# Sums for the odd output weights: moved from the mixing stage into the query and key stage, at two steps a piece

## The chip, the cores and the metric

One core of a Trainium2 chip runs the whole kernel. The metric is the device time of one execution in microseconds (us). TensorE (PE) multiplies, VectorE (DVE) and ScalarE (ACT) prepare operands and empty PSUM, and every transfer between device memory and on-chip memory is issued by one queue, that of SyncE (SP). Each engine runs its own list of instructions strictly in order, and so does SP: a transfer that has to wait holds up all that stand behind it.

## The reference, cut to what matters

Two residual layers over 1024 tokens of width 1024, batch 1, all in float32.

```python
def even_layer(x, cos, sin, mem_n, ...):          # layer 0
    proj = rmsnorm(x, g_norm) @ w_in              # 1024 x 6656
    qk, v_a, x_b, q_m, z = split(proj)            # qk: 3 dilations x (query, key) x 4 heads x 128
    a_out = dilated_attention_mixer(qk, v_a, cos, sin)
    b_out = multiscale_pool(x_b, w_pool, pool_scale)
    m_out = memory_attention(q_m, mem_n, w_mem_kv)
    return x + (concat(a_out, b_out, m_out) * silu(z)) @ w_out     # w_out: 1536 x 1024

def odd_layer(x, mem_n, ...):                     # layer 1
    u, v, q_m, z = split(rmsnorm(x, g_norm) @ w_in)
    c_out = chunked_spatial_gating(u, v, ln_g, ln_b, w_s, b_s)     # the "mixing" of chunks of 128 tokens
    m_out = memory_attention(q_m, mem_n, w_mem_kv)
    return x + (concat(c_out, m_out) * silu(z)) @ w_out            # w_out: 1536 x 1024
# the end: rmsnorm(x, final_norm_g)
```

## The kernel before

**Products.** A float32 matmul is made of three passes over operands that are split into a high and a low part: high times high, high times low, low times high. `split` makes the parts: ACT writes the high part (line 111, tile `wh`), DVE subtracts to get the low part (line 112, tile `wl`). On top of that, the large products use a seven-product scheme in place of eight block products. For that, sums and differences of weight blocks and of activation blocks are needed.

**Pairs.** The input projections go in pairs of 128 output columns. `pair` issues one pair: seven products in the order 1, 7, 6, 4, 5, 2, 3, each of 12 matmuls of 128x128x512 (4 slices of depth, 3 passes), so 84 matmuls. After each product one *step* runs (`step`), and each step advances a few generators by one `yield`: the preparation of the next pair's weights (`prep_steps`: four sums `sw` in lines 147 to 161, seven splits), the two side generators `side[0]` and `side[1]`, and the attention units. DVE empties the PSUM banks (tiles `pj`) of a pair in four instructions: `u` or `u2` (line 278) after product 6, `X` (line 282) after product 4, `X` (line 286) after product 5, `X` (line 291) after product 2. Product 3 adds into the bank that line 286 reads, so it cannot start before that instruction is done. The raw weights of a pair come in two transfers of 512 KB (`raw_pair`, line 107), two pairs ahead, into three buffers.

**Stages.** After the memory keys come the query and key stage (six batches of two pairs, here pairs 0 to 11; `project_batch`), the attention stage of layer 0 (its first pairs are called pairs 12 and 13 here, tiles `xb` and `zb`), the output product of layer 0, the value product of layer 1, a memory stage, the mixing stage of layer 1 (four rounds `g` = 0, 2, 4, 6 of two pairs each; `mixed` is side generator 1) and the output product of layer 1. In the query and key stage the rotation of a batch (`rotate`: a shuffle in line 708 and three instructions in lines 710, 712 and 714) is side generator 1 of the batch behind it.

**Sums of output weights.** The output products and the value product use the seven-product scheme too. The sums of their weights are made ahead and put into device memory (`wt_d`, `ws_d`), from where the later stages read them. `sums_of` does this in pieces of 512 KB: two loads of 256 KB into a tile `wt`, four DVE instructions of 128x256 (line 204), one store of 512 KB. There are two `wt` buffers, so the load of piece n+2 waits until the store of piece n has landed. There are 8 pieces for the value product, 12 for the even output weights and 12 for the odd ones. The first 20 are side generator 0 of the query and key stage, the last 12 that of the mixing stage. A piece takes three steps: one yield after the loads, one after two of the four sums, one after the store. Below, o0 to o11 are the odd pieces in their order.

**What sets the order.** The code is written for all engines at once; the framework that lowers it then lists each engine's instructions by its own estimate of when each is ready. So a change in one place can move instructions of any engine that stand near it. The lists are fixed before the run.

Of the kernel before, what the change touches and what calls it, by code (L numbers as in the profile page):

```python
# [47 lines left out]
def trunk(ctx, tc, A):  # L48
# [4 lines left out]
    def pool(name, side="left"):  # L53
        st = ExitStack()
        return st, st.enter_context(tc.tile_pool(name=name, bufs=1, side=side, reuse_waits="tile"))
# [24 lines left out]
    def at(t, off, ap):  # L80
        return bass.AP(tensor=t.tensor, offset=t.offset + off, ap=ap)
# [92 lines left out]
    H1 = ((4, 5, 6, 7, 0, 1), (8, 9, 10, 11, 2, 3))  # L174
    H2 = ((8, 9, 10, 11, 0, 1), (2, 3, 4, 5, 6, 7))
    sub, add = OP.subtract, OP.add

    def out_pieces(l, w, h):
        for j in range(6):
            for c in range(2):  # L180
                src = [at(w, h[q][j] * 131072 + c * 256, [[1024, 128], [512, 2], [1, 256]]) for q in range(2)]
                dst = at(wt_d, ((l * 6 + j) * 128) * 2048 + c * 256, [[2048, 128], [512, 4], [1, 256]])
                yield src, dst, ((3, 3, 1, sub), (1, 1, 0, sub), (0, 3, 0, add), (2, 2, 0, sub))

    def v_pieces(w):
        for c in range(2):
            for q in range(4):
                src = [at(w, h * 524288 + c * 131072 + q * 256, [[1024, 128], [262144, 2], [1, 256]]) for h in range(2)]
                dst = at(ws_d, c * 524288 + q * 256, [[4096, 128], [1024, 4], [1, 256]])
                yield src, dst, ((3, 2, 3, add), (2, 0, 2, sub), (0, 3, 0, sub), (1, 1, 0, sub))  # L190

    def sums_of(p, pieces):
        prev = None
        for src, dst, f in chain(pieces, ((None, None, None),)):
            t = None
            if src:
                t = p.tile([128, 4, 256], F32, name="wt", tag="wt", bufs=2)
                for q in range(2):
                    D.dma_start(t[:, 2 * q:2 * q + 2, :], src[q])
            yield  # L200
            if prev:
                tt, dd, ff = prev
                for n, (o, x, y, op) in enumerate(ff):
                    V.tensor_tensor(tt[:, o, :], tt[:, x, :], tt[:, y, :], op=op)  # L204
                    if n == 1:
                        yield
                D.dma_start(dd, tt)
                yield
            prev = (t, dst, f)

    side = [iter(()), iter(())]
# [90 lines left out]
    def pair_tiles(p, src, idx, tag, bufs, permuted=False):  # L302
        xs = [p.tile([128, 1024], F32, name="X", tag=tag, bufs=bufs) for _ in range(2)]

        def dst(blk, half):
            if permuted:
                d = xs[blk].rearrange("p (r q) -> p r q", r=4)[:, :, half * 128:half * 128 + 128]
                return d, lambda t: t.rearrange("p (q r) -> p r q", r=4)
            return xs[blk][:, half * 512:(half + 1) * 512], lambda t: t
        pair(src, idx, dst)  # L310
        return xs
# [348 lines left out]
    sq, pq = pool("pq", "right")  # L660
# [43 lines left out]
    def rotate(bi, g, C, S_):  # L704
# [10 lines left out]
        for i in range(4):  # L715
            D.dma_start(qk_d[bi, i, 96:128, :], g[i * 32:(i + 1) * 32, :])

    sums = sums_of(pq, chain(v_pieces(A["wov"]), out_pieces(0, A["woute"], H1)))
    for bi in range(6):
        side[1] = project_batch(bi, rope_tables if bi == 0 else None)  # L720
        if bi == 0:
# [159 lines left out]
    def y_out(p, l, r, o, z):  # L881
        t = gate(p, z, "t", 2)
        V.scalar_tensor_tensor(o, o, 0.5, t, op0=OP.mult, op1=OP.mult)
        D.dma_start(y_d[l][r], o)
# [116 lines left out]
    def out_first(p, w, h):  # L1001
        return [to_ops(p, "ow", OW, half_raw(w[h[0][j], :, :512])) for j in range(6)]
# [275 lines left out]
    def mixed(g, out):  # L1278
        vgs = []
        for q in range(2):  # L1280
            vg = pc_.tile([128, 8, 128], F32, name="vg", tag="vg", bufs=2)
            D.dma_start(vg, at(v2_d, (g + q) * 128, [[1024, 128], [128 * 1024, 8], [1, 128]]))
            vgs.append(vg)
        yield
        for q, vg in enumerate(vgs):
            for n in range(8):
                V.tensor_scalar(vg[:, n, :], vg[:, n, :], lr[:, 0, n:n + 1], lr[:, 1, n:n + 1], op0=OP.mult, op1=OP.add)
            mx = pc_.tile([128, 8, 128], F32, name="mx", tag="mx", bufs=2)
            out.append(mx.rearrange("p n t -> p (n t)"))
            yield  # L1290
            for a in range(2):
                pm_ = bank(("s", "s", "tr", "pv")[q * 2 + a])
                for n in range(4):
                    T.matmul(pm_[:, n * 128:(n + 1) * 128], vg[:, a * 4 + n, :], wsT[:, g + q, :], start=True, stop=True)
                V.scalar_tensor_tensor(mx[:, a * 4:a * 4 + 4, :], pm_.rearrange("p (n t) -> p n t", n=4),
                                       smalls[:, 4 + g + q:5 + g + q], Bg[:, g + q:g + q + 1, :].to_broadcast([128, 4, 128]),
                                       op0=OP.mult, op1=OP.add)
                yield

    spre, ppre = pool("ppre", "right")  # L1300
    side[0] = sums_of(ppre, out_pieces(1, A["wouto"], H2))
    mx = []
    side[1] = mixed(0, mx)
    next(side[1])
    for g in range(0, 8, 2):
        us = pair_tiles(pb, A["wo"], (g, g + 1), "X", 4)
        for _ in side[1]:
            pass
        for q in range(2):
            V.tensor_tensor(us[q], us[q], mx[q], op=OP.mult)  # L1310
        if g < 6:
            mx = []
            side[1] = mixed(g + 2, mx)
            next(side[1])
        if g == 6:
            for _ in side[0]:
                pass
            spre.close()
            sc.close()
            sr.close()  # L1320
            sln.close()
            sw_, pw = pool("ow1", "right")
            first = out_first(pw, A["wouto"], H2)
        for q, z in enumerate(pair_tiles(pb, A["wo"], (12 + g, 13 + g), "X", 4)):
            y_out(pb, 1, g + q, us[q], z)
# [86 lines left out]
```

## Time and profile before

| | |
|---|---|
| three timed runs | 1290.73, 1290.88 and 1292.93 us, median 1290.88 us |
| the profiled execution | 1293.09 us in all, 1291.1 us of it the span from the first to the last instruction |
| PE busy | 1249.8 us (97%), 6008 matmuls |
| DVE busy | 1043.2 us (81%) |
| ACT busy | 578.5 us (45%) |
| transfers | 226.10 MB, 52.6% of the time of the 16 DMA engines |

Busy time of PE says little of its pace, since a matmul starts before the one ahead of it has ended: matmuls of 128x128x512 last 0.39 us each and start every 0.23 us. What PE loses shows as a longer distance between two starts. A row of the timeline has the start, the duration, the engine, the line, the operation, the tiles as out<-in, and in brackets, where the engine sat idle ahead of it, for how long and until what.

### The profile page before, as it was taken

What the parts mean: (1) busy time and instruction counts of PE and PEld (TensorE: products, weight loads), DVE (VectorE), ACT (ScalarE), POOL (GpSimd) and SP (SyncE); (2) the same over time, 40 slices, a digit from 0 to 9 for tenths busy, and PEclk for the clock granted to TensorE, in tenths of its full rate; (3) what the DMA queues carried; (4) which work ended last, traced back from release to release, by engine and by line L of the source; (5) the groups of instructions that cost most, each with busy time, mean ns of one, the idle gap of its engine ahead of it and who ended that gap; (6) DMA issues with size and microseconds to landing.
All of it is one profiled execution on the core that took longest, in us unless ns stands there. A gap on an engine that the chain in (4) does not pass through costs nothing.

```text
span 1291.1 us, 17491 instructions
## 1 busy us (share of the span) xinstructions
PE 1249.8 (97%) x6008; PEld 1024.2 (79%) x6008; DVE 1043.2 (81%) x1968; ACT 578.5 (45%) x1155; POOL 48.3 (4%) x51
## 2 busy tenths in 40 slices
PE   6999999999999999999999999999999999999997
PEld 6888888788877877787788787877888887888786
DVE  5998777877676787887977967998878999667976
ACT  6734323233345554455553644632656232243552
POOL 1162000000000000000000001000000000000001
PEclk9999999999999999999999999999999999999999
DMA  7824765767447656533259534524032677239633
GB/s 271 286 99 135 249 207 177 224 198 243 147 149 223 221 161 223 183 114 112 77 191 347 179 108 182 194 96 131 18 98 89 201 240 236 66 115 334 236 114 130
DMA packets 128990, 226.10 MB, mean 175 GB/s; under 512 B 11139, under 2 KB 79363, under 8 KB 128902
## 3 DMA queue, kind: packets, MB, share of 16 engines
q1 hardware_dynamic: 128902, 224.99, 52.6%
q8 instruction: 47, 0.77, 0.3%
q14 instruction: 41, 0.34, 0.1%
HBM read 158.79 MB, written 63.01 MB: 172 GB/s over the span
## 4 chain that ended last, share of the span: by engine, by line
PE 61%; DVE 18%; DMA 13%; issue 4%; ACT 2%; POOL 1%; SPq 1%; DVEq 0%; POOLq 0%; ACTq 0%
PE pj L265 33%; DMA raw<-wt_d 2%; DVE wl L112 2%; DMA sl<-qk_d 2%; PE pv L490 2%; PE pj L432 2%; PE pj L433 2%; PE pj L434 2%; PE s L465 2%; DMA raw<-in_we_dram 1%; PE s L777 1%; DMA ct<-rr_d 1%; PE pj L1045 1%; DVE wt L204 1%; PE pj L1043 1%
## 5 line engine op out<-in xcount | busy, mean ns | idle before, releaser
L265 PE MATMUL pj<-hTh,wh 128*128 128x512 f32 x544 | 217.7, 400 | 6.1 <-DVE u L278 4.2
L265 PE MATMUL pj<-hTh,wl 128*128 128x512 f32 x544 | 215.1, 396 | 0.0
L265 PE MATMUL pj<-hTl,wh 128*128 128x512 f32 x544 | 213.8, 393 | 0.0
L111 ACT ACTIVATE wh<-sw 128x512 fp32r<-128x512 f32 x136 | 85.8, 631 | 220.7 <-PE pj L265 184.6
L111 ACT ACTIVATE wh<-raw 128x512 fp32r<-128x512 f32 x106 | 66.8, 630 | 147.0 <-PE pj L265 136.8
L265 PEld LDWEIGHTS pj<-hTh,wh 128*128 128x128 f32 x544 | 102.6, 189 | 30.2 <-DVE u L278 6.7
L112 DVE TENSOR_TENSOR wl<-sw,wh 128x512 fp32r<-128x512 f32 x136 | 93.3, 687 | 32.8 <-ACT wh L111 31.5
L265 PEld LDWEIGHTS pj<-hTh,wl 128*128 128x128 f32 x544 | 102.6, 189 | 20.9
L265 PEld LDWEIGHTS pj<-hTl,wh 128*128 128x128 f32 x544 | 102.7, 189 | 19.6
L111 ACT ACTIVATE owh<-raw 128x512 fp32r<-128x512 f32 x84 | 52.3, 628 | 79.0 <-DMA raw<-wt_d 36.5
L112 DVE TENSOR_TENSOR owl<-raw,owh 128x512 fp32r<-128x512 f32 x84 | 57.4, 690 | 34.0 <-ACT owh L111 33.8
L112 DVE TENSOR_TENSOR wl<-raw,wh 128x512 fp32r<-128x512 f32 x106 | 72.6, 685 | 8.9 <-ACT wh L111 7.7
L1045 PE MATMUL pj<-owh,oyl 128*128 128x512 f32 x192 | 76.3, 398 | 0.9 <-DVE oyl L112 0.9
L1043 PE MATMUL pj<-owh,oyh 128*128 128x512 f32 x192 | 76.4, 398 | 0.0
L1044 PE MATMUL pj<-owl,oyh 128*128 128x512 f32 x192 | 75.7, 394 | 0.0
L204 DVE TENSOR_TENSOR wt<-wt 128x256 f32<-128x256 f32 x128 | 51.6, 421 | 9.1 <-DMA wt<-in_woute_dram 2.6
L265 PE MATMUL pj<-t2h,wh 128*128 128x512 f32 x136 | 54.5, 401 | 0.0
L265 PE MATMUL pj<-t0l,wh 128*128 128x512 f32 x136 | 53.8, 395 | 0.0
L265 PE MATMUL pj<-t0h,wh 128*128 128x512 f32 x136 | 53.7, 395 | 0.0
L265 PE MATMUL pj<-t2l,wh 128*128 128x512 f32 x136 | 53.6, 394 | 0.0
L265 PE MATMUL pj<-t1h,wh 128*128 128x512 f32 x136 | 53.5, 394 | 0.0
L377 POOL TENSOR_TENSOR rs<-ss,nhalf 128x1 f32<-128x1 f32 x18 | 12.0, 668 | 1108.0 <-DVE ss L376 1108.0
(364 smaller groups left out, 3098.1 us busy)
## 6 DMA issues: line engine op xcount, KB each, us to landing
raw<-in_we_dram SPq DMA_DIRECT2D x44, 512.0 KB
wt_d<-wt SPq DMA_DIRECT2D x24, 512.0 KB
y<-y_d SPq DMA_DIRECT2D x24, 512.0 KB
raw<-wt_d SPq DMA_DIRECT2D x48, 256.0 KB
raw<-in_wo_dram SPq DMA_DIRECT2D x24, 512.0 KB
y_d<-X SPq DMA_DIRECT2D x20, 512.0 KB
qk_d<-X SPq DMA_DIRECT2D x24, 384.0 KB
sl<-qk_d SPq DMA_DIRECT2D x16, 512.0 KB
```

The costliest lines, as they stand in the source:

```text
L111: S.activation(hi, raw, AF.Copy)
L112: e.tensor_tensor(lo, raw, hi.bitcast(F32), op=OP.subtract)
L204: V.tensor_tensor(tt[:, o, :], tt[:, x, :], tt[:, y, :], op=op)
L265: T.matmul(ps, w[:, k, :], m, start=(start and k == 0 and w is hi and m is B[k][0]), stop=(k == 3 and w is lo), skip_group_check=True)
L432: T.matmul(ps, hi, wh[c], start=(k == 0), stop=False)
L433: T.matmul(ps, hi, wl[c], start=False, stop=False)
L434: T.matmul(ps, lo, wh[c], start=False, stop=(k == 7))
L465: T.matmul(s3[:, a, :], qs[i][:, (pr * 2 + a) * 128:(pr * 2 + a + 1) * 128], kvp[j][:, :256], start=n == 0, stop=n == 2)
L490: T.matmul(pv[:, pr * 256:(pr + 1) * 256], kvp[i][:, 256 + kb * 128:384 + kb * 128], PT[j][:, kb * 256:(kb + 1) * 256], start=(kb == 0 and ...
L1043: T.matmul(ps, yh[:, c], wh, start=start, stop=False, skip_group_check=True)
L1044: T.matmul(ps, yh[:, c], wl, start=False, stop=False, skip_group_check=True)
L1045: T.matmul(ps, yl[:, c], wh, start=False, stop=stop, skip_group_check=True)
```

## The change

`sums_of` loses its first yield, so that a piece takes two steps: the loads of piece n+1 and the first half of the sums of piece n in one, the second half and the store of piece n in the next. The 12 odd pieces join the chain of the query and key stage (32 pieces in all, with the same two `wt` buffers), and the mixing stage has no side generator 0 any more, nor the pool that it used and the loop that ran it dry ahead of the last round. The arithmetic of each piece is the same.

```diff
--- before.py
+++ after.py
@@ -197,7 +197,6 @@
                 t = p.tile([128, 4, 256], F32, name="wt", tag="wt", bufs=2)
                 for q in range(2):
                     D.dma_start(t[:, 2 * q:2 * q + 2, :], src[q])
-            yield
             if prev:
                 tt, dd, ff = prev
                 for n, (o, x, y, op) in enumerate(ff):
@@ -715,7 +714,7 @@
         for i in range(4):
             D.dma_start(qk_d[bi, i, 96:128, :], g[i * 32:(i + 1) * 32, :])
 
-    sums = sums_of(pq, chain(v_pieces(A["wov"]), out_pieces(0, A["woute"], H1)))
+    sums = sums_of(pq, chain(v_pieces(A["wov"]), out_pieces(0, A["woute"], H1), out_pieces(1, A["wouto"], H2)))
     for bi in range(6):
         side[1] = project_batch(bi, rope_tables if bi == 0 else None)
         if bi == 0:
@@ -1297,8 +1296,6 @@
                                        op0=OP.mult, op1=OP.add)
                 yield
 
-    spre, ppre = pool("ppre", "right")
-    side[0] = sums_of(ppre, out_pieces(1, A["wouto"], H2))
     mx = []
     side[1] = mixed(0, mx)
     next(side[1])
@@ -1313,9 +1310,6 @@
             side[1] = mixed(g + 2, mx)
             next(side[1])
         if g == 6:
-            for _ in side[0]:
-                pass
-            spre.close()
             sc.close()
             sr.close()
             sln.close()
```

The lists of PE, DVE, ACT and SP are the same as before up to about 200 us into the run; they differ from there to the first units of the attention stage, are the same again from there on (PE from its row 1726, DVE from its row 577), and differ once more in the mixing stage, where the sums are missing. Three places follow. In them the number behind a tile's name tells instances apart. Pair 11 has the tiles `X_3125` and `X_3124` before and `X_3218` and `X_3217` now; pair 12 has `X_3295` and `X_3294` before and `X_3391` and `X_3390` now.

**Place 1: DVE, pair 11.** Before, from the `u2` of pair 11 to its last `X`; the low parts of the weights of pair 12 (`wl_3144`, `wl_3164`, `wl_3186`) stand between the instructions that empty the banks, and `wl_3144` is that of its first product:

```order
L278 TENSOR_TENSOR u2_3183<-pj_3126,m7_3161 128x512
L112 TENSOR_TENSOR wl_3144<-raw_3083,wh_3143 128x512
L282 TENSOR_TENSOR X_3125<-pj_3128,u2_3183 128x4x128
L112 TENSOR_TENSOR wl_3164<-sw_3147,wh_3163 128x512
L161 TENSOR_TENSOR sw_3223<-raw_3083,sw_3169 128x512
L286 TENSOR_TENSOR X_3125<-pj_3126,m7_3161 128x4x128
L112 TENSOR_TENSOR wl_3186<-sw_3169,wh_3185 128x512
L291 TENSOR_TENSOR X_3124<-pj_3127,m1_3141 128x4x128
```

Now, from the third of these instructions of pair 11 (line 285, which was 286) to the low part of the first weights of pair 12 (`wl_3237`). `rw` and `rg` are the rotation of batch 4, `wt_3068` is piece o9:

```order
L285 TENSOR_TENSOR X_3218<-pj_3219,m7_3257 128x4x128
L707 STREAM_SHUFFLE rw_3073<-rg_3034 128x1024
L709 TENSOR_TENSOR rg_3034<-rg_3034,Ct_1293 128x1024
L711 TENSOR_TENSOR rw_3073<-rw_3073,St_1294 128x1024
L203 TENSOR_TENSOR wt_3068<-wt_3068 128x256
L713 TENSOR_TENSOR rg_3034<-rg_3034,rw_3073 128x1024
L203 TENSOR_TENSOR wt_3068<-wt_3068 128x256
L290 TENSOR_TENSOR X_3217<-pj_3220,m1_3234 128x4x128
L203 TENSOR_TENSOR wt_3068<-wt_3068 128x256 x2
L147 TENSOR_TENSOR sw_3240<-raw_3171,raw_3169 128x512
L151 TENSOR_TENSOR sw_3263<-raw_3169 128x512
L112 TENSOR_TENSOR wl_3237<-raw_3171,wh_3236 128x512
```

The first weights of pair 12 have moved from ahead of the second `X` of pair 11 to behind its last one, and the rotation and piece o9 stand in between.

**Place 2: SP, around the raw weights of pair 13.** Before (`raw_3225` and `raw_3227` are those of pair 13, `raw_3083` is the second half of pair 12's):

```order
L107 DMA raw_3083<-in_we_dram 128x1024
L716 DMA qk_d_65<-rg_2957 32x1024 x4
L107 DMA raw_3225<-in_we_dram 128x1024
L699 DMA rg_3263<-X_2966 32x1024
L700 DMA qk_d_65<-X_2966 96x1024
L699 DMA rg_3263<-X_3125 32x1024
L700 DMA qk_d_65<-X_3125 96x1024
L107 DMA raw_3227<-in_we_dram 128x1024
L699 DMA rg_3263<-X_3124 32x1024
L700 DMA qk_d_65<-X_3124 96x1024
L107 DMA raw_3497<-in_we_dram 128x1024
```

Now (`wt_3068`, `wt_3117` and `wt_3163` are o9, o10 and o11; `raw_3321` and `raw_3323` are the raw weights of pair 13):

```order
L206 DMA wt_d_74<-wt_3068 512x1x256
L715 DMA qk_d_65<-rg_3034 32x1024 x2
L199 DMA wt_3163<-in_wouto_dram 128x2x256 x2
L206 DMA wt_d_74<-wt_3117 512x1x256
L715 DMA qk_d_65<-rg_3034 32x1024 x2
L206 DMA wt_d_74<-wt_3163 512x1x256
L107 DMA raw_3321<-in_we_dram 128x1024
L107 DMA raw_3323<-in_we_dram 128x1024
L698 DMA rg_3359<-X_3043 32x1024
L699 DMA qk_d_65<-X_3043 96x1024
L698 DMA rg_3359<-X_3044 32x1024
```

The raw weights of pair 13 stood between the stores of pairs 10 and 11; now they stand behind the store of the last piece, o11, whose load needs the buffer of o9 and so waits until the store of o9 has landed.

**Place 3: DVE, pair 12.** Before, around its `u2` and its three `X`:

```order
L112 TENSOR_TENSOR wl_3314<-raw_3227,wh_3313 128x512
L278 TENSOR_TENSOR u2_3373<-pj_3296,m7_3333 128x512
L112 TENSOR_TENSOR wl_3336<-sw_3317,wh_3335 128x512
L161 TENSOR_TENSOR sw_3464<-raw_3227,sw_3341 128x512
L112 TENSOR_TENSOR wl_3376<-sw_3341,wh_3375 128x512
L112 TENSOR_TENSOR wl_3416<-raw_3225,wh_3415 128x512
L282 TENSOR_TENSOR X_3295<-pj_3298,u2_3373 128x512
L286 TENSOR_TENSOR X_3295<-pj_3296,m7_3333 128x512
L112 TENSOR_TENSOR wl_3461<-sw_3339,wh_3460 128x512
L291 TENSOR_TENSOR X_3294<-pj_3297,m1_3311 128x512
```

Now its `u2` stands seven rows further up than the rows shown, right behind the sums of o11. Between it and the two `X` that follow stand ten rows for pair 13 (four sums and six splits, of which the last four are shown), the rotation of batch 5 and the first two sums for pair 14, which read `raw_3593` and `raw_3595`:

```order
L112 TENSOR_TENSOR wl_3472<-sw_3437,wh_3471 128x512
L112 TENSOR_TENSOR wl_3512<-raw_3321,wh_3511 128x512
L112 TENSOR_TENSOR wl_3557<-sw_3435,wh_3556 128x512
L112 TENSOR_TENSOR wl_3611<-raw_3323,wh_3610 128x512
L707 STREAM_SHUFFLE rw_3368<-rg_3359 128x1024
L709 TENSOR_TENSOR rg_3359<-rg_3359,CtB_1295 128x1024
L711 TENSOR_TENSOR rw_3368<-rw_3368,StB_1296 128x1024
L713 TENSOR_TENSOR rg_3359<-rg_3359,rw_3368 128x1024
L147 TENSOR_TENSOR sw_3730<-raw_3595,raw_3593 128x512
L151 TENSOR_TENSOR sw_3790<-raw_3593 128x512
L281 TENSOR_TENSOR X_3391<-pj_3394,u2_3469 128x512
L285 TENSOR_TENSOR X_3391<-pj_3392,m7_3429 128x512
```

The instructions that empty the banks of pair 12 now stand behind work that needs the raw weights of pairs 13 and 14. Behind them in both lists come the first attention units; on PE the first of their matmuls (line 824, `s<-sl`) stands at the same row in both, 1617, with as many matmuls ahead of it, and on SP the first load that it needs (`sl`) stands in both behind the stores of the rotation of batch 5.

## Rows read from the trace of the kernel before

**Rows 1.** Busy time (us, times) by stretch: key stage, then mixing stage

```profile
core 0: us, PE busy (x) PEld busy (x) DVE busy (x) ACT busy (x) POOL busy (x), PEclk, DMA share, GB/s
117.66:350.88 233.22, 231.54 (x1026) 190.44 (x1024) 177.99 (x295) 72.14 (x123) 0.00 (x0) 1.00 0.66 208
1000.00:1100.00 100.00, 97.43 (x466) 80.88 (x466) 95.06 (x198) 29.21 (x47) 0.00 (x0) 0.98 0.68 222
```

**Rows 2.** Timeline of PE in the last round of the mixing stage

```profile
1092.11 0.39 PE L265 MATMUL pj<-hTh,wh 128*128 128x512 f32 x1
1094.95 0.50 PE L265 MATMUL pj<-hTh,wh 128*128 128x512 f32 x1 [2.46 <-DVE u L278]
...
1096.25 0.63 PE L265 MATMUL pj<-hTh,wl 128*128 128x512 f32 x1
...
1099.63 0.40 PE L265 MATMUL pj<-hTh,wl 128*128 128x512 f32 x1
```

**Rows 3.** The page's group of the sums of weights on DVE

```profile
L204 DVE TENSOR_TENSOR wt<-wt 128x256 f32<-128x256 f32 x128 | 51.6, 421 | 9.1 <-DMA wt<-in_woute_dram 2.6
```

**Rows 4.** Timeline of DVE, sums that waited for their load

```profile
232.23 1.34 DVE L204 TENSOR_TENSOR wt<-wt 128x256 f32<-128x256 f32 x3 [1.36 <-DMA wt<-in_woute_dram]
...
1083.47 0.43 DVE L204 TENSOR_TENSOR wt<-wt 128x256 f32<-128x256 f32 x1 [1.33 <-DMA wt<-in_wouto_dram]
```

**Rows 5.** Timeline of SP, loads and stores of pieces

```profile
228.10 2.57 SPq L199 DMA_DIRECT2D wt<-in_woute_dram  x4
...
1059.15 1.21 SPq L199 DMA_DIRECT2D wt<-in_wouto_dram  x2
1060.45 0.56 SPq L207 DMA_DIRECT2D wt_d<-wt  x1
...
1065.02 1.20 SPq L199 DMA_DIRECT2D wt<-in_wouto_dram  x2
...
1077.31 1.20 SPq L199 DMA_DIRECT2D wt<-in_wouto_dram  x2
1079.28 0.56 SPq L207 DMA_DIRECT2D wt_d<-wt  x1
...
1084.68 1.21 SPq L199 DMA_DIRECT2D wt<-in_wouto_dram  x2
```

**Rows 6.** Timeline of PE, pair 11 to the first attention unit

```profile
345.44 0.39 PE L265 MATMUL pj<-hTh,wh 128*128 128x512 f32 x1
...
350.88 0.39 PE L265 MATMUL pj<-hTh,wh 128*128 128x512 f32 x1
...
375.14 0.49 PE L824 MATMUL s<-sl 128*128 128x128 f32 x2
```

**Rows 7.** Timeline of DVE, pairs 11 and 12

```profile
345.64 1.07 DVE L286 TENSOR_TENSOR X<-pj,m 128x512 f32<-128x512 f32 x1 [0.32 <-PE pj L265]
346.62 0.69 DVE L112 TENSOR_TENSOR wl<-sw,wh 128x512 fp32r<-128x512 f32 x1
...
353.76 0.69 DVE L147 TENSOR_TENSOR sw<-raw 128x512 f32<-128x512 f32 x1 [1.49 <-DMA raw<-in_we_dram]
...
354.97 0.68 DVE L112 TENSOR_TENSOR wl<-raw,wh 128x512 fp32r<-128x512 f32 x1
...
355.58 1.35 DVE L708 STREAM_SHUFFLE rw<-rg 128x1024 f32<-128x1024 f32 x1
356.97 1.23 DVE L710 TENSOR_TENSOR rg<-rg,CtB 128x1024 f32<-128x1024 f32 x1
358.11 0.68 DVE L112 TENSOR_TENSOR wl<-sw,wh 128x512 fp32r<-128x512 f32 x1
```

**Rows 8.** Timeline of SP, end of the query and key stage

```profile
350.07 0.35 SPq L107 DMA_DIRECT2D raw<-in_we_dram  x1
...
361.70 1.70 SPq L716 DMA_DIRECT2D qk_d<-rg  x4
369.23 0.35 SPq L107 DMA_DIRECT2D raw<-in_we_dram  x1
...
371.04 0.43 SPq L813 DMA_DIRECT2D sl<-qk_d  x1
```

## The prediction

> **What bounds the kernel now.** I read three views: busy time by stretch, the timeline of PE, and the timelines of DVE and SP at the places where the lists of instructions differ. Over the query and key stage PE has 231.5 of 233.2 us busy and DVE 178.0 [rows 1]; the pace of PE shows better in its starts. From 345.44 to 350.88 us stand 24 matmuls, 0.227 us each [rows 6], so a product takes 2.72 us and a pair 19.04 us, and PE is the bound there as long as DVE empties its banks and delivers weights in time. In the mixing stage DVE is busy for 95.1 of 100 us [rows 1], and there PE loses time once: in the last round it stands from 1092.11 to 1094.95 us, until DVE has done the `u` of that pair, and from 1096.25 to 1099.63 us its matmuls start 0.42 us apart in place of 0.23 [rows 2]. That is the lower of its two clock levels (1.2 in place of 2.4 GHz), and the mean granted clock of that stretch is 0.98, against 1.00 in the query and key stage [rows 1].
>
> **What the change takes away.** Twelve pieces leave the mixing stage, 48 instructions of 421 ns on DVE [rows 3], 20.2 us. PE waits for DVE only in the place above, so the gain is what PE lost there: 2.84 - 0.23 = 2.61 us of standing, and 3.38 - 8 x 0.227 = 1.56 us of slow matmuls. DVE's delay is that of the sums: one waited 1.33 us for its load [rows 4], and three more ran ahead of the `u`, 1.33 + 4 x 0.42 = 3.0 us, more than the 2.61. **-4.2 us**, between 0 (DVE is held by its other work) and the same 4.2, since nothing else of PE's waits in these rows is larger.
>
> **What it adds, on average.** The 20.2 us go to the query and key stage: 178.0 + 20.2 = 198.2 us of DVE in 233.2, 85%. That alone would cost nothing. What costs is where the work stands in lists that are run in order, so the three places of the section on the change are costed row by row. DVE starts instructions that follow each other closer than they last: 0.605 us apart for a sum or split of 128x512 (two from 353.76 to 354.97), 1.39 for the shuffle, 1.14 for a rotation's product, 0.98 for an `X` [rows 7]. A `wt` sum gets its 0.42 [rows 3].
>
> **Place 1, the first weights of pair 12.** The `X` of line 286 in pair 11 starts at 345.64 us, when PE has done product 5 [rows 7]; it can't start sooner. Now the rows from it to `wl_3237` follow: two `X` (1.96), the shuffle (1.39), three instructions of the rotation (3.42), four sums of o9 (1.68), two sums of weights (1.21) and the split to its end (0.69): 10.35 us, which is 355.99 us. PE wants these weights with the third matmul of pair 12, at 350.88 + 2 x 0.227 = 351.33 us [rows 6]. So **PE stands for 4.7 us**; before, these weights were made while PE worked on pair 11.
>
> **Place 2, the raw weights of pair 13.** The store of o9 can go when its last sum is done, 345.64 + 8.45 = 354.1 us. The load of o11 waits until that store has landed. From the issue of a store to that of a load that waited for it, it took 4.57 us (1060.45 to 1065.02) and 5.40 us (1079.28 to 1084.68) [rows 5]; I take 5.0: 359.1 us. From the issue of a load to the first sum that waited for it, it took 4.13 us (228.10 to 232.23) with nothing in front, and 6.16 us (1077.31 to 1083.47) with other loads and stores behind it [rows 4, 5]; here nothing stands in front, so I take 4.2: 363.3 us. DVE is there earlier, at 356.0 + 4 x 0.42 + 7 x 0.605 = 361.9 us, and waits. Two sums, a split and two sums (2.3 us) end at 365.6 us, the store of o11 takes SP 0.56 us [rows 5], and the raw weights of pair 13 are issued at 366.2 and 366.55 us. One took 3.69 us from issue to the DVE instruction that waited for it, 350.07 to 353.76 [rows 7, 8]: 370.2 us.
> The Trainium skill, page "DMA: Bandwidth & Descriptors", section "Anatomy of one DMA", fits a transfer as 2.0 us plus its bytes at 436 GB/s, measured on transfers issued from GpSimd, which is an estimate of 3.2 us for 512 KB. The rows here show 3.7 to 6.2 us, so the trace does not agree; by the page's figure the sum below would be 1.9 us smaller, 1301.0 us.
>
> **Place 3, the banks of pair 12.** Ten rows for pair 13 (6.05 us) and the rotation (1.39 + 3.42 = 4.8) end at 381.1 us; two sums of pair 14 and two `X` follow, to 384.3 us. Only then may product 3 of pair 12 start. Up to there PE has, from 355.5 us on, six products of pair 12 and two of pair 13, eight times 2.72 = 21.8 us, to about 377.3 us. So **PE stands a second time, for 7 us**. Then come the stores of the rotation on SP (1.70 us from 381.1) and, 1.81 us after these as before (369.23 to 371.04), the first `sl` at 384.6 us; its matmul followed 4.10 us after its issue, 371.04 to 375.14 [rows 6, 8]: 388.7 us. PE has as many matmuls ahead of it as before, when it was at 375.14 us: **+13.6 us**. Bounds: with the shorter price of the store and `sl` in time, six matmuls behind 383.9 us, +10.1; with both longer prices, +16.0.
>
> **The clock and what follows.** After a stop of 2.5 us the slow matmuls cost 1.56 us [rows 2]. Two longer stops come: 0 to 3.1 us; the first is covered by the wait for DVE that comes behind it, so I take one, **+1.6**. Behind 388.7 us the attention units have the same work as before, but fewer matmuls stand between them. No row prices that: 0 to 4.1 us (one more load of `sl` in full); nearer to 0, as these loads are issued ahead: **+1.0**. From there on the lists are those of before, and a delay stays.
>
> **Sum.** -4.2 + 13.6 + 1.6 + 1.0 = +12.0 us. The profiled execution took 1293.09 us with a span of 1291.1, so 1305.1 us on its own scale; it lies 2.2 us above the median of the timed runs, on whose scale the forecast is 1290.9 + 12.0 = **1302.9 us**.
>
> **Rivals.**
> *The chain of pieces falls behind earlier.* Each load of a piece waits on SP for a store two pieces back. Four such cycles took 25.53 us (1059.15 to 1084.68), 6.38 each, the last 7.37 [rows 5]. In the new list DVE has about three pieces a pair, one per 6.35 us. At 6.38 the chain holds; at 7.37 it loses 1.0 us a piece, and over the nine pieces o0 to o8, of which some three are covered by loads that run ahead, +6: 1309 us. For it: 208 GB/s flow already in this stage [rows 1], and the pieces come closer. It decides above 6.4 us a cycle.
> *Only the first stop counts.* If the raw weights of pair 13 land 7 us sooner than worked out, the `X` of pair 12 come in time: 4.7 + 1.6 - 4.2 = +2.1, 1293 us. Both transfers would have to take half of what rows 5 show.
> *Faster.* Nothing in the new order reaches PE, and the mixing stage alone counts: -4.2, 1286.7 us. For it speaks the 85% of DVE. It holds if the rows of place 1 take less than 5.7 us (345.64 to 351.33) in place of 10.35, and those of place 3 are covered as well; the durations speak against it.
>
> **How the numbers follow.** The forecast, 1297 to 1309 us (its own bounds): 0.55. The chain earlier: 0.18, and both it and a longer tail, beyond 1313: 0.08. Only the first stop: 0.10. Faster: 0.09. A range of 1293 to 1312 us leaves out the fast case and the slowest, some 0.2. A measurement of this kernel tells about 0.2%, 2.6 us, from no change: faster by more 0.09; within it 0.06, most of the case of +2.1; slower 0.85.
>
> **What would show it.** In the mixing stage no stop of PE for a `u` near the last round, and the clock at 1.00: right on the gain. At the start of pair 12 a stop of PE of 4 to 5 us that ends with the split of line 112; on SP the raw weights of pair 13 right behind the store of o11, later than 362 us, with DVE idle on them; the first matmul of line 824 some 13 us later than 375.14. Wrong would be: PE going through pair 12 without a stop of over 2 us, or stops in pairs 6 to 10 that end with a `wt` load (the first rival), or a mixing stage whose PE still waits for DVE.

## The result, and the profile after

The changed kernel takes 1306.33 us (median of five runs, 1306.05 to 1310.51) against 1290.88 us (five runs): a ratio of 1.0115, 95% interval 1.0092 to 1.0138. It is slower by 15.4 us. The profiled execution took 1306.15 us with a span of 1304.4 us, 13.3 us more than the span of before.

Where they went is told by matmuls with the same number in PE's list, which has 6008 in both kernels; the times are their starts in the two traces.

| matmul of PE's list | before | after | after minus before |
|---|---|---|---|
| 1101st (pair 6) | 238.97 | 239.82 | +0.85 |
| 1501st (pair 11) | 331.84 | 330.49 | -1.35 |
| 1688th (first attention unit, L824, now L823) | 375.14 | 393.44 | +18.29 |
| 1701st | 378.34 | 397.67 | +19.33 |
| 3401st (output product of layer 0) | 722.89 | 739.15 | +16.25 |
| 5001st (mixing stage) | 1054.03 | 1070.41 | +16.38 |
| 5201st (behind its last round) | 1100.10 | 1113.67 | +13.57 |
| 6008th (last) | 1282.92 | 1296.31 | +13.39 |

So the whole loss, 46.50 us that became 67.19, lies in 200 matmuls from pair 11 to the first attention units. I call this the *stretch*; +20.7 us is what it cost here.

Busy time by stretch, the rows that answer to [rows 1]: the query and key stage, two short stretches inside the loss, and the mixing stage.

```profile
core 0: us, PE busy (x) PEld busy (x) DVE busy (x) ACT busy (x) POOL busy (x), PEclk, DMA share, GB/s
117.66:350.88 233.22, 230.93 (x1023) 190.07 (x1022) 185.59 (x322) 70.40 (x121) 0.00 (x0) 1.00 0.77 242
352.10:358.90 6.80, 4.96 (x12) 3.80 (x13) 6.77 (x15) 2.30 (x4) 0.00 (x0) 0.50 0.59 174
382.80:396.50 13.70, 6.59 (x15) 4.70 (x16) 6.50 (x12) 1.98 (x4) 0.00 (x0) 0.50 0.58 168
1017.00:1117.00 100.00, 98.35 (x479) 82.19 (x478) 83.78 (x160) 29.84 (x48) 0.00 (x0) 1.00 0.32 109
```

In the query and key stage PE is as busy as before, and DVE for 185.6 us, 80% of this window and not the 85% of the prediction; ten of the 48 sums ran behind it. In the mixing stage DVE fell from 95.1 to 83.8 us in 100, and the clock is at its upper level. The two short rows are at the lower level, 1.2 GHz, 20.5 us together.

Timeline of PE, its waits from pair 11 to the first attention unit with the matmul ahead of the longest, and the one wait left in the last round of the mixing stage (compare [rows 2, 6]).

```profile
350.89 0.50 PE L264 MATMUL pj<-hTh,wh 128*128 128x512 f32 x1 [1.21 <-ACT wh L111]
...
353.94 0.79 PE L264 MATMUL pj<-t1h,wh 128*128 128x512 f32 x1 [2.31 <-ACT wh L111]
...
373.50 0.50 PE L264 MATMUL pj<-hTh,wl 128*128 128x512 f32 x1 [0.52 <-DVE wl L112]
...
379.38 0.39 PE L264 MATMUL pj<-t0h,wl 128*128 128x512 f32 x1
387.65 0.79 PE L264 MATMUL pj<-t1h,wh 128*128 128x512 f32 x1 [7.88 <-DVE X L281]
...
393.44 0.80 PE L823 MATMUL s<-sl 128*128 128x128 f32 x2 [2.26 <-DMA sl<-qk_d]
...
1110.13 0.50 PE L264 MATMUL pj<-hTh,wh 128*128 128x512 f32 x1 [1.25 <-DVE u L277]
```

Timeline of DVE from the `X` of pair 11 to those of pair 12 (compare [rows 7]).

```profile
344.28 1.05 DVE L285 TENSOR_TENSOR X<-pj,m 128x512 f32<-128x512 f32 x1 [1.67 <-PE pj L264]
...
353.68 0.68 DVE L112 TENSOR_TENSOR wl<-raw,wh 128x512 fp32r<-128x512 f32 x1
...
371.55 0.69 DVE L147 TENSOR_TENSOR sw<-raw 128x512 f32<-128x512 f32 x1 [6.47 <-DMA raw<-in_we_dram]
...
377.25 0.69 DVE L112 TENSOR_TENSOR wl<-sw,wh 128x512 fp32r<-128x512 f32 x1 [0.67 <-ACT wh L111]
380.24 0.69 DVE L112 TENSOR_TENSOR wl<-raw,wh 128x512 fp32r<-128x512 f32 x1 [2.30 <-ACT wh L111]
380.86 0.01 DVE L707 LOAD_MASK_SELECT rw<-rg  x1
380.86 1.28 DVE L707 STREAM_SHUFFLE rw<-rg 128x1024 f32<-128x1024 f32 x1
...
386.91 0.68 DVE L281 TENSOR_TENSOR X<-pj,u 128x512 f32<-128x512 f32 x1
387.51 0.68 DVE L285 TENSOR_TENSOR X<-pj,m 128x512 f32<-128x512 f32 x1
```

Timeline of SP over the same time (compare [rows 8]): the store of o9, the load of o11, its store, the raw weights of pair 13, the first `sl`.

```profile
352.59 0.58 SPq L206 DMA_DIRECT2D wt_d<-wt  x1
...
356.01 1.21 SPq L199 DMA_DIRECT2D wt<-in_wouto_dram  x2
...
363.60 0.57 SPq L206 DMA_DIRECT2D wt_d<-wt  x1
364.27 1.55 SPq L107 DMA_DIRECT2D raw<-in_we_dram  x2
...
389.07 0.43 SPq L812 DMA_DIRECT2D sl<-qk_d  x1
```

The chain of the prediction is there: rotation and o9 ahead of the first weights of pair 12, raw weights of pair 13 behind the store of o11, `X` of pair 12 behind all of that, PE waiting 7.9 us for `X`, then `sl`. One row was not in it, the split at 380.24 us, which waited 2.30 us for ACT. ACT's own timeline says for what:

```profile
376.59 0.62 ACT L111 ACTIVATE wh<-sw 128x512 fp32r<-128x512 f32 x1
379.58 0.63 ACT L111 ACTIVATE wh<-raw 128x512 fp32r<-128x512 f32 x1 [2.36 <-PE pj L264]
```

That `wh` had to wait for a weight buffer (`w2`, ten tiles, so the high and low parts of five products), which PE frees as it ends a product. PE's last matmul before its long stop starts at 379.38 us, and this `wh` starts 0.20 us later. So the lists made what I call the *circle*: PE waits for `X`; `X` stands on DVE behind a split; the split needs a buffer that PE frees only with the last product it can do without that `X`. It does not lock, since PE can still do that product, but the stop is what runs from there: 0.20, `wh` and its split to 380.86, the rotation to 385.71, two sums, and the first `X`, whose end at 387.6 releases PE.

### The profile page after: what moved, and what is told of

Read it like the earlier page. It is cut to its first block, busy times and chain, and to the rows that moved or that the text cites. A ratio compares the mean times of both kernels' runs of the same rounds, so it can differ in the third digit from the quotient of the medians.

```text
span 1304.4 us, 17478 instructions
## 1 busy us (share of the span) xinstructions
PE 1251.6 (96%) x6008; PEld 1026.2 (79%) x6008; DVE 1045.3 (80%) x1968; ACT 578.5 (44%) x1155; POOL 48.4 (4%) x51
## 4 chain that ended last, share of the span: by engine, by line
PE 71%; DVE 12%; DMA 10%; issue 3%; ACT 2%; SPq 1%; POOL 1%; DVEq 0%; POOLq 0%; ACTq 0%
PE pj L264 36%; PE pj L1044 3%; PE pj L1042 3%; PE pj L1043 3%; DMA ct<-rr_d 2%; PE pv L489 2%; PE pj L431 2%; PE pj L432 2%; PE pj L433 2%; PE s L464 2%; DMA raw<-in_we_dram 1%; DMA sl<-qk_d 1%; DVE wl L112 1%; PE s L776 1%; PE s L1044 1%
## 5 line engine op out<-in xcount | busy, mean ns | idle before, releaser
L264 PE MATMUL pj<-t1l,wh 128*128 128x512 f32 x136 | 53.5, 394 | 0.0
```

Of the source, the lines that this page charges most:

```text
L264: T.matmul(ps, w[:, k, :], m, start=(start and k == 0 and w is hi and m is B[k][0]), stop=(k == 3 and w is lo), skip_group_check=True)
```

## The experiments

The theory was that the order of SP and DVE at pairs 11 to 13 costs the time (places 1 to 3); the rivals were the added load itself (DVE at 85%, or the transfers), the closer steps, and a cost for each piece. The ratio is to the kernel before on the same chip, with its 95% interval. The stretch is from the 1501st to the 1701st matmul, read from one profiled execution of each kernel.

| kernel | median us | before us | ratio | stretch, over the 46.50 of before |
|---|---|---|---|---|
| changed kernel | 1306.33 | 1290.88 | 1.0115 (1.0092 to 1.0138) | +20.7 |
| two steps alone | 1290.80 | 1290.66 | 1.0004 (0.9989 to 1.0019) | -0.1 |
| move alone, three steps | 1322.89 | 1290.66 | 1.0254 (1.0235 to 1.0272) | +32.6 |
| pieces on POOL's queue | 1390.21 | 1290.66 | 1.0780 (1.0760 to 1.0801) | -0.2 |
| sums from pair 0 on | 1305.07 | 1290.66 | 1.0125 (1.0107 to 1.0144) | +14.5 |
| `X` ahead | 1302.06 | 1290.26 | 1.0094 (1.0071 to 1.0116) | +15.7 |
| both of these | 1296.71 | 1290.26 | 1.0063 (1.0040 to 1.0087) | +8.8 |
| raw weights on POOL's queue | 1316.11 | 1290.26 | 1.0200 (1.0169 to 1.0230) | -0.1 |
| three pieces moved | 1287.52 | 1290.26 | 0.9982 (0.9965 to 0.9999) | -0.1 |
| six pieces moved | 1295.07 | 1290.03 | 1.0046 (1.0029 to 1.0064) | +4.9 |
| transfers alone | 1300.53 | 1290.03 | 1.0087 (1.0059 to 1.0114) | +13.4 |
| sums alone | 1295.01 | 1290.03 | 1.0043 (1.0020 to 1.0065) | -0.5 |

**Two steps alone.** The kernel before, less one line:

```diff
-            yield
```

> The kernel before with the first yield of sums_of taken out and nothing moved: the 12 odd pieces stay in the mixing stage. Theory (the loss comes from the order of SP and DVE at pairs 11 to 13, which only the move changes): the lists around pairs 11 to 13 are those of before, so the first attention matmul stays at 375 us, within 2 us; in the mixing stage the pieces end earlier, so part or all of PE's stop near 1092 us goes: 1286.7 to 1290.9 us. Rival (pieces that come closer together are what costs, whatever their number): stops in pairs 6 to 10, over 1293 us.

No measurable difference, and nothing in the stretch; the rival is out. The stops that it removed in pair 6 and near 1092 us did not show in the median.

**The move alone.** The changed kernel with that line put back:

```diff
+            yield
```

> The changed kernel with the yield put back: 32 pieces of three steps, 96 steps where the five batches have 70, so some 9 pieces are left when the last pair ends. Theory (transfers that wait on SP hold the raw weights and sl behind them): about 5 pieces at some 6.4 us stand between the last raw weights and the first sl, so the first attention matmul comes later than the 393 us of the changed kernel, and the time is 10 to 30 us longer than its 1306: 1316 to 1336 us. Rival (it is the sums' 20 us of DVE in this stage): the same work in the same stage, so about 1306 us, within 4.

As the theory had it. SP's timeline shows the first `sl` behind the last stores, PE's the stop:

```profile
403.10 2.98 SPq L207 DMA_DIRECT2D wt_d<-wt  x2
...
408.31 0.43 SPq L813 DMA_DIRECT2D sl<-qk_d  x1
```

```profile
406.15 0.80 PE L265 MATMUL pj<-t1h,wh 128*128 128x512 f32 x1 [28.32 <-DVE X L282]
...
411.77 0.49 PE L824 MATMUL s<-sl 128*128 128x128 f32 x2 [2.09 <-DMA sl<-qk_d]
```

**Pieces on POOL's queue.** In `sums_of` of the changed kernel:

```diff
-                    D.dma_start(t[:, 2 * q:2 * q + 2, :], src[q])
+                    G.dma_start(t[:, 2 * q:2 * q + 2, :], src[q])
...
-                D.dma_start(dd, tt)
+                G.dma_start(dd, tt)
```

> The changed kernel with the loads and stores of all 32 pieces issued from POOL's queue in place of SP's. The DVE work, the bytes, the two buffers and the two steps are the same, and the waits of a load for a store two pieces back now hold POOL, which does nothing else there. The DVE list around pairs 11 and 12 becomes that of before, word for word. Theory (SP's waits and the order that follows from them cause the loss): no stop of PE over 2 us in pairs 11 to 13, first attention matmul at 374 to 377 us, the mixing stage as in the changed kernel (2.8 us gained): 1286 to 1290 us. Rival (85% of DVE, or 208 GB/s and more of transfers in the stage, cause it): the stops stay somewhere, 1298 us or more.

A miss of 100 us. The stretch itself was clean, with the first attention matmul running without a wait, but the loads came late in every pair before it. Waits of DVE, then of PE, from 130 to 430 us (total, times, longest):

```profile
DVE wt L203 <- DMA wt<-in_wouto_dram: 37.9, 8, 9.5
DVE wt L203 <- DMA wt<-in_woute_dram: 32.9, 7, 11.1
...
PE pj L264 <- DVE u L277: 70.7, 11, 10.1
```

A sum that waits on DVE holds the `u2` behind it, and PE with it. This is the first rival of the prediction, the chain that falls behind, and shows what it would have looked like.

**Sums from pair 0 on.**

```diff
...
+    side[0] = sums
...
```

> The changed kernel with the sums started with pair 0 in place of pair 2, so that the last piece is stored about one pair earlier and ahead of the raw weights of pairs 12 and 13. Theory: these raw weights land in time, the 6.5 us that DVE waited for them go, and so does the stop at the start of pair 12; but the list of DVE still has the rows for pair 13, the rotation and two sums of pair 14 ahead of the X of pair 12, so a shorter second stop of 3 to 6 us stays: 1290 to 1298 us. Rival (DVE's load alone): about 1306 us. Rival (only the last pieces' place matters, the X list does not): 1287 us.

A miss: 1305.07. DVE no longer waited for the raw weights of pair 13, yet PE's stop for `X` was still there:

```profile
385.12 0.79 PE L264 MATMUL pj<-t1h,wh 128*128 128x512 f32 x1 [4.16 <-DVE X L281]
...
390.58 0.79 PE L824 MATMUL s<-sl 128*128 128x128 f32 x2 [1.94 <-DMA sl<-qk_d]
```

ACT's timeline has the circle again: the last `wh` for pair 13 starts at 380.77 us, 0.20 behind the start of PE's last matmul before the stop (380.57):

```profile
380.77 0.63 ACT L111 ACTIVATE wh<-raw 128x512 fp32r<-128x512 f32 x1 [2.88 <-PE pj L264]
```

The stop is shorter than 8 us because part of the rotation ran ahead of that split. So a stop at the `X` needs no late raw weights.

The stretch of +14.5 flatters this kernel: part of its loss moved ahead of the stretch. A stop of the kind of place 1 stands there two pairs earlier,

```profile
314.46 0.50 PE L264 MATMUL pj<-hTh,wh 128*128 128x512 f32 x1 [1.21 <-ACT wh L111]
```

and its 1501st matmul comes 2.4 us later than before, where that of the changed kernel comes 1.35 us sooner. At the 1701st the changed kernel lies 19.3 us behind and this one 16.8. The ratios, 1.0125 and 1.0115, show no gain.

**`X` ahead.** The changed kernel with steps of pair 12 queued behind `u2` and behind each `X`; `issue_after` sets the order of the list:

```diff
-        def step():
+        def step(behind=None):
+            if behind is not None and i in (12,):
+                with tc.issue_after(behind.ins):
+                    step()
+                return
...
-        V.tensor_tensor(d, f(e), f(u2), op=OP.add)
-        step()
+        step(V.tensor_tensor(d, f(e), f(u2), op=OP.add))
...
```

> The changed kernel with one edit of the order alone: in pair 12 the preparation steps behind u2 and behind each X are queued on DVE behind that instruction. The transfers and the work are the same. The list of DVE then has four rows for pair 13 and the rotation ahead of the X of pair 12, and no longer ten rows, the rotation and two sums of pair 14. Theory (place 3, the X behind rows that wait for the raw weights of pair 13 and for free weight buffers, is the larger part of the loss): the raw weights still land at about 371.5 us, then some 3 us of rows and 4.8 us of rotation, X near 380 us in place of 388; the stop of 8 us shrinks to 0 to 3, the first attention matmul comes some 6 us earlier than 393.4: 1298 to 1301 us. Rival (the late raw weights alone set the loss, the place of X in the list does not): 1304 to 1308 us as before the edit.

The raw weights were as late as ever, and the stop went down to 1.79 us:

```profile
370.59 0.69 DVE L147 TENSOR_TENSOR sw<-raw 128x512 f32<-128x512 f32 x1 [6.35 <-DMA raw<-in_we_dram]
```

```profile
380.59 0.50 PE L268 MATMUL pj<-t1h,wh 128*128 128x512 f32 x1 [1.79 <-DVE X L284]
...
386.52 0.79 PE L823 MATMUL s<-sl 128*128 128x128 f32 x2 [2.78 <-DMA sl<-qk_d]
```

The `X` now stand ahead of the splits that need buffers; six rows for pair 13 remained ahead of them, not four as I had counted. At 1302.06 us the time is 1 us above the theory's range: the first attention matmul came 6.9 us sooner, but the stretch shrank by 5.0 only.

**Both.** The last two edits together:

> Both at once: the sums start with pair 0, and in pair 12 the preparation steps are queued behind u2 and each X. Theory (with the raw weights in time and the X not held, only the stop at the start of pair 12 and its slow clock stay): first attention matmul at 379 to 385 us, 1293 to 1299 us. Rival (something else in the fuller stage takes the time, and neither place matters by itself): 1303 us or more.

1296.71 us, as the theory had it; PE has no stop at the `X` any more. With the two edits the stretch makes a square: +20.7 with neither, +14.5 with the early start, +15.7 with `X` ahead, +8.8 with both. The effects nearly add: 6.2 and 5.0 alone, 11.9 together. Counted from the start of the run to the 1701st matmul, which takes in what moved ahead of the stretch, the four lie 19.3, 16.8, 13.5 and 11.1 us behind the kernel before: 2.5 and 5.9 alone, 8.2 together. The 8.8 that stay hold the stops at the start of pair 12 (1.21 and 0.84), one for `u2` (1.66) and the one for `sl` (2.57). The raw weights of pair 13 were not in time here, against what was expected; DVE waited for them ahead of that `u2`:

```profile
366.29 0.69 DVE L147 TENSOR_TENSOR sw<-raw 128x512 f32<-128x512 f32 x1 [3.41 <-DMA raw<-in_we_dram]
```

I did not take the rest apart further.

**Raw weights on POOL's queue.** The changed kernel with `G.dma_start` in place of `D.dma_start` for `raw`:

```diff
...
+            e = G if 2 <= i <= 13 else D
+            second = load_raw(s[y], e)
+            rawp[i] = (load_raw(s[x], e), second)
```

> The changed kernel with the raw weights of pairs 2 to 13 issued from POOL's queue in place of SP's; the pieces stay on SP with their waits. So no raw weights can be held behind a store or a load of a piece. Theory (SP's one queue is the root: it makes the raw weights of pairs 12 and 13 late, and the order of DVE follows): no stop of PE over 2 us at the start of pair 12 and a stop under 3 us ahead of the first attention matmul, 1287 to 1295 us. Rival (the raw weights are late through the traffic, whatever the queue, or POOL's queue is slower in itself, which the kernel with all pieces on it suggests): stops in pairs 2 to 11 in their place, over 1300 us.

The stretch is clean, but the time is that of the rival: from 130 to 350 us DVE waited 35.0 us for raw weights, after 9.0 in the changed kernel.

```profile
DVE sw L148 <- DMA raw<-in_we_dram: 35.0, 10, 5.4
```

Whether the queue or the order it brought made them late is open. The kernel shows only that raw weights of pairs 12 and 13 that don't stand behind pieces leave the stretch as it was. That holds although its sums were there too: the last 14 of the 48 ran inside the stretch, from 349.5 to 368.7 us, 13 of them in pair 11, where the changed kernel has 20, ten in each of pairs 11 and 12. So sums on DVE in pair 11 cost nothing by being there.

**Transfers alone, and sums alone.** The changed kernel with the odd pieces' sums left out:

```diff
-                yield src, dst, ((3, 3, 1, sub), (1, 1, 0, sub), (0, 3, 0, add), (2, 2, 0, sub))
+                yield src, dst, () if l else ((3, 3, 1, sub), (1, 1, 0, sub), (0, 3, 0, add), (2, 2, 0, sub))
...
+                if not ff:
+                    yield
```

> The changed kernel without the 48 sums of the odd pieces on DVE: their weights are loaded and stored as they are, so that part of the computation is left out. The transfers, the two buffers, the two steps and SP's waits stay, and DVE has the load of before in the query and key stage. The list of DVE still has the X of pair 12 behind the rows for pair 13, the rotation and two sums of pair 14. Theory (the order that SP's waits bring costs the time, not the sums on DVE): most of the loss stays, a stop of 3 us or more ahead of the X of pair 12, 1297 to 1305 us. Rival (DVE at 85% is what costs): no stop, 1285 to 1290 us.

And the kernel of two steps with 48 sums on a spare tile behind the even pieces:

```diff
...
+    def sums_alone():
+        for _ in range(12):
+            for n in range(4):
+                V.tensor_tensor(spare[:, 0, :], spare[:, 0, :], spare[:, 1, :], op=OP.add)
+                if n == 1:
+                    yield
+            yield
...
```

> The counterpart: the kernel of two steps with the odd pieces in the mixing stage, and in the query and key stage behind the even pieces 48 sums of the same shape on a spare tile, which are added work that no result uses, without any transfer. DVE has the 198 us of the changed kernel in that stage. The rows around the X of pair 12 stand as in the kernel before. Theory: no stop of PE over 2 us in pairs 2 to 13, the time of the kernel with two steps alone, 1288 to 1293 us. Rival (DVE at 85%): 1297 us or more.

Without the odd pieces' sums the stretch still loses 13.4 of the 20.7 us, as the theory had it: the larger part needs the transfers and the order that comes with them, not the sums. What the traffic costs apart from the order was not tested; the kernel with `X` ahead has the same transfers and loses 5.0 us less by its order alone. In the kernel without sums the raw weights of pair 13 held DVE for 1.50 us only, and the circle made the stop all the same, PE's and DVE's rows:

```profile
382.23 0.80 PE L266 MATMUL pj<-t1h,wh 128*128 128x512 f32 x1 [6.55 <-DVE X L283]
```

```profile
363.05 0.69 DVE L147 TENSOR_TENSOR sw<-raw 128x512 f32<-128x512 f32 x1 [1.50 <-DMA raw<-in_we_dram]
...
376.15 0.69 DVE L112 TENSOR_TENSOR wl<-raw,wh 128x512 fp32r<-128x512 f32 x1 [2.07 <-ACT wh L111]
```

The kernel with the sums alone says less than was meant. With no load to wait for, its 48 sums went far forward in the list. The view of their tile:

```profile
L723 DVE TENSOR_TENSOR spare<-spare x48: 412/422/431, 121.9 to 190.5; 128x256 f32<-128x256 f32 x48
```

So they ran in pairs 0 to 3, where the odd pieces' sums of the changed kernel ran from 285 to 363 us. That its stretch loses nothing is no test of sums at pairs 11 to 13, and the 7.3 us between 13.4 and 20.7 may be theirs or those of the order they bring; that is open, though the 14 sums in the clean stretch of the kernel above speak for the order. At 1295.01 us it came between the theory's range and the rival's. Where the sums stood, they delayed an `X` and a `u2`, in pairs 1 and 2:

```profile
156.86 0.50 PE L264 MATMUL pj<-hTh,wh 128*128 128x512 f32 x1 [1.44 <-DVE X L285]
...
172.86 0.50 PE L264 MATMUL pj<-hTh,wh 128*128 128x512 f32 x1 [2.09 <-DVE u L277]
```

So added work on DVE costs where it stands ahead of what PE waits for; this kernel does not show what its share of the stage costs by itself.

**Three and six pieces moved.** The other pieces go back to the mixing stage, as before but in two steps:

```diff
...
+    odd = list(out_pieces(1, A["wouto"], H2))
+    sums = sums_of(pq, chain(v_pieces(A["wov"]), out_pieces(0, A["woute"], H1), odd[:3]))
...
+    side[0] = sums_of(ppre, odd[3:])
...
```

> The changed kernel with only the first three odd pieces in the query and key stage, the other nine in the mixing stage in two steps each. It is the largest number for which DVE's rows around the X of pairs 11 and 12 stand as before. Theory (the loss comes when the chain of pieces reaches pairs 11 and 12): no stop of PE over 2 us in pairs 11 to 13, first attention matmul within 3 us of 375: 1286 to 1290 us. Rival (each piece costs its share, a quarter of the loss): 1293 to 1296 us.

> The changed kernel with six odd pieces moved, six left in the mixing stage. DVE's list has the X of pair 12 behind eight rows for pair 13 and the rotation of batch 5, and the raw weights of pair 13 on SP behind the store of the last but one piece. Theory (the loss sets in when X and raw weights of pairs 12 and 13 are reached): a stop at the X of pair 12 of 1 to 5 us, 1289 to 1296 us. Rival of a share for each piece between three moved (1287.5) and twelve (1306): 1293.7 us. Rival (only the last three pieces do it): 1286 to 1288.5 us.

Three pieces: 1287.52 us, the fastest kernel here, though its interval against the one before nearly touches 1. PE's waits from 117 to 395 us are the first three rows, from 1000 to 1130 us the last:

```profile
PE pj L264 <- DVE u L277: 0.9, 2, 0.5
PE s L777 <- DMA sl<-qk_d: 0.6, 1, 0.6
PE s L824 <- DMA sl<-qk_d: 0.4, 1, 0.4
...
PE s L1294 <- issue: 0.6, 1, 0.6
```

The stops near 245 and 1092 us are gone, nothing came in their place. Six pieces cost 4.9 us in the stretch, with a stop of 1.82 us for `X`. The six were profiled in an execution 6.8 us above their median, so their stretch is read with care. Their time lies in the theory's range, but only 1.4 us above the 1293.7 of an even share for each piece from three to twelve, so what speaks for the theory is the stop and not the time. Against the kernel before on the same chip three pieces make -2.7 us, six +5.0 and twelve +15.4: no fixed price that holds from the first piece on.

## Why the prediction was right, and where it was not

**Sign, place and sum held.** 1302.9 us was forecast, 1306.3 measured. On the spans +12.0 was forecast and +13.3 measured; the remaining 2.2 us are those by which the profiled execution of before lay above its median. But terms that were off cancelled: place 3 was 4.7 us too small, and the tail came out 4.1 us lower than forecast.

**The gain in the mixing stage, -4.2:** -2.8 (from 16.38 to 13.57 in the table). The stop shrank from 2.61 to 1.41 us (1108.49 to 1110.13 us) and the clock did not fall after it. The prediction had all of the stop go, and named a wait of PE for DVE in this stage as a sign of being wrong; on this point it was. The `u` was not late through the sums alone: without them DVE's rows still run from 1101.2 us to the `u` at 1109.4 with no idle time.

**Place 1, a stop of 4.7 us:** right in size. From the `X` of pair 11 to the end of the first low part it took 344.28 to 354.36, 10.08 us for 10.35 forecast. PE stood twice, 1.37 and 2.48 us from start to start less 0.23. But neither stop ended with the split of line 112, which was to be the sign; both ended with a high part of ACT, and the prediction costed no row of ACT:

```profile
349.72 0.60 ACT L294 ACTIVATE X<-pj 128x512 f32<-128x512 f32 x1 [12.66 <-PE pj L264]
350.22 0.62 ACT L111 ACTIVATE wh<-raw 128x512 fp32r<-128x512 f32 x1
353.26 0.63 ACT L111 ACTIVATE wh<-sw 128x512 fp32r<-128x512 f32 x1 [2.42 <-DVE sw L147]
```

The first `wh` stands behind the last `X` of pair 11, which waits for PE; only the second follows a row of place 1 on DVE. The low part was ready 0.17 us before the matmul that reads it (354.53), so DVE's rows would have held PE about as long.

**Place 2:** the raw weights were issued at 364.27 and 364.94 us (366.2 and 366.55 forecast), but DVE could use them at 371.55 (370.2): 6.6 us from the second issue, in place of 3.69. The fit of the Trainium skill (page "DMA: Bandwidth & Descriptors", section "Anatomy of one DMA"), made for transfers issued from GpSimd, gives an estimate of 3.2 us and is further off; the trace of these transfers from SyncE disagrees with it here too. Six more transfers are issued within 6 us behind them; that these slowed them is argued, not shown.

**Place 3, +13.6 with bounds of 10.1 to 16.0:** +18.3, outside the bounds, and the step that failed. It counted the ten rows for pair 13 by their length alone, 6.05 us from the landing of the raw weights. They took 9.3 us (371.55 to 380.86), mainly since two splits wait for ACT, which waits for PE, the last of them for a weight buffer: 3.3 of the 4.7 us that were missing, with 1.35 more from place 2. PE was released by the first `X` already, for a bank of pair 13, and not by that of line 285. The length of the stop, 7 us forecast and 8.04 measured, came out by luck. In the forecast it lies between two things that do not touch, PE running out of products and DVE's rows that start with the raw weights; in the traces PE's last product releases the last split, and the stop runs round the circle. The kernel that starts early and the one without sums show that raw weights in time, or 1.5 us late, leave 4.3 and 6.7 us of it; the one with `X` ahead, that late ones leave 2.0. What the late raw weights cost by themselves is not isolated: the early start takes 6.2 of the 20.7 us from the stretch, but 2.5 at the 1701st matmul.

**The clock, +1.6:** two low stretches of 6.8 and 13.7 us. The first lies ahead of the matmul at 373.50 us, which waited 0.52 us for a low part made of the late raw weights; without the low stretch PE would have waited there longer, so I count nothing for it, as in the forecast (argued from that row, not tested). In the second, the six matmuls from 387.65 to 390.55 us took 2.90 us in place of 1.36, but PE then stood for `sl` for 2.26 us, which covers them. From the 1688th to the 1701st it took 4.23 us for 3.20: +1.0, within the bounds.

**The tail, +1.0:** from the 1701st to the 3401st matmul 3.1 us came back instead, 2.0 of them between the 2301st and the 2501st and 2.1 between the 3301st and the 3401st, less what was lost in between; why is open. With the terms as measured, -2.8 + 18.3 + 1.0 - 3.1 makes +13.4 us.

**Ahead of pair 11, nothing was forecast:** a stop in pair 6 went, 2.2 us between the 1101st and the 1501st matmul, and earlier pairs lost some of it. The rival of a chain that falls behind before pair 11 did not occur; the rival with only the first stop failed because the second did not hang on the raw weights alone: with them in time, 4.3 us of it stayed.

## What to carry to other kernels

When work is moved into a stage, its share of an engine's time says little: ask at which place of an in-order list it ends, and what is queued behind its last waits. Before pricing a row by its length, ask what it needs beside its data: an instruction that empties a bank must not stand behind one that needs a buffer which the waiting engine frees. Part of a move can be worth more than all of it; here three of twelve pieces fit ahead of the point where the order turns over.

## What was not expected of the hardware

In the changed kernel the granted clock stayed at 1.2 GHz for 6.8 us from the second of two stops on, of 1.4 and 2.5 us, and for 13.7 us around a stop of 8.0 us that was followed by one of 2.3 (its row's idle time); before, it was 3.4 us after one of 2.6. After the stop of 1.4 us in the mixing stage it did not fall at all.

Pieces loaded and stored from POOL's queue came far later than from SP's: DVE waited 11.1 us for one, where the longest such wait in the kernel before is 1.4 us. The Trainium skill (page "DMA: Bandwidth & Descriptors", section "SWDGE vs HWDGE vs iDMA") has transfers from GpSimd described by software and those from SyncE by hardware with a faster setup; the direction agrees, but a wait of this size follows from no figure there, and the cause within that queue was not looked into.
